# A grouped RMS norm whose factor is spread by a store to DRAM and a broadcast read, in place of matmuls with diagonals

## The chip, the cores and the metric

The kernel runs on one core of a Trainium2 chip. The metric is the device time of one execution in microseconds; the time of a kernel is the median of its runs. Smaller is better.

## The reference

The kernel is one step of a hybrid decoder trunk: an RMS norm of the input, one large input projection, two branches, a gated merge, an output projection, a residual and a last RMS norm. The change lies in branch A, a Mamba-2 state space branch (SSD) with 64 heads in 8 groups. Its output `y` is gated with `z`, normalised over the 512 channels of each group, and projected:

```python
def gated_group_rms_norm(y, z, w):
    g = y.astype(jnp.float32) * jax.nn.silu(z.astype(jnp.float32))
    shp = g.shape
    g = g.reshape(shp[:-1] + (SSD_GROUPS, shp[-1] // SSD_GROUPS))
    g = g * lax.rsqrt(jnp.mean(g * g, axis=-1, keepdims=True) + EPS)
    return (g.reshape(shp) * w.astype(jnp.float32)).astype(y.dtype)
...
    y = jnp.concatenate(ys, axis=1) + d_skip[:, None] * xs
    y = gated_group_rms_norm(y.reshape(bsz, length, D_INNER), z, ssd_norm_w)
    y_a = y @ w_ssd_out
```

There are 320 tokens that count (256 of the prompt and 8 x 8 samples) and 16 meta tokens ahead of them. For each group and each token one number, the factor 1/sqrt(mean + eps), multiplies all 512 channels.

## The kernel before, in words

Channels lie on the 128 partitions and tokens along the free dimension, so a group's `y` is four tiles `ys` of 128 x 320. The sum over 512 channels is a sum over four tiles and over partitions, and the factor, one number for each token, has to stand on all partitions.

**Projections.** Nearly all of TensorE's work (PE) is projections. A weight block of 128 x 1024 comes by DMA from SP (`wraw`, line 80), ACT rounds it to fp32r (`whi`, L82), DVE makes the remainder (`wlo`, L84), each in three buffers. `mm` (L90, L91, L94) then makes high by high, high by low and low by high products into a PSUM tile `pj`, of which there are two. A projection of the input takes two blocks, 48 matmuls into one `pj`; a block of the branch's own output projection (`out_units`, L563) serves two tiles of 12 matmuls, and each is added to `ya` by DVE (L574), which frees the `pj`.

**The weave.** For each group g a generator `ssd` makes the branch's small steps; it stops at each `yield`. `weave` (L594) runs the projections of the group's gate `z` (4 units), the output projection of group g−1 (8 units) and the convolution inputs of group g+1 (6 units) one after the other, and lets `ssd` advance between units so that NSTEP steps are spread over them; what is left runs at the end. Group 0 has no output projection to weave in, and group 7 has gate units (8) in place of the next group's convolutions. A scheduler then sets the order on each engine within what the buffers and the data allow. All engines run their instructions in order, and SP issues its DMAs in order too.

**One group's steps.** Three chunks of tokens (L436 to L518): transposes (L444), the decay weights `W` read from DRAM (L441) and worked by DVE (L456), the chunk's products (L475, L493, L470), the state (L504). In the third chunk the sampled states enter (L481, L483) and POOL multiplies eight states `h` with their decays (L486). Then `ys` is multiplied with the gate `zs` by DVE (L528), ACT squares it into `zs` (L529), POOL adds the four squares (L531). Two passes over the sampled states follow (L533 to L552): selections by matmuls (L535 to L541), state products (L548) in four `sg` tiles of which two buffers exist, added to `h` by DVE (L549) and stored (L551).

**The norm.** Last comes `rstd` (L106). It sums the squares over partitions for three spans of 112 tokens, each by a matmul with a column of ones (L112); DVE scales and adds eps (L116); POOL raises to −1/2 (L117); now each span's factors stand one to a partition. DVE multiplies the identity with them (three diagonals `rs_d`, L122), and a matmul of ones with each diagonal (L123) puts the factors on all partitions, in PSUM. DVE multiplies `ys` with weight and factor (L557), ACT rounds (`yh`, L558), DVE makes the remainder (`yl`, L559). The same `rstd` serves the first norm (L223) and the last (L646).

Of the kernel before, what the change touches and what calls it, by code (L numbers as in the profile page):

```python
# [7 lines left out]
F32 = mybir.dt.float32  # L8
F32R = mybir.dt.float32r
AF = mybir.ActivationFunctionType  # L10
ALU = mybir.AluOpType
PSUM = bass.MemoryType.PSUM

P = 128
T = 336
META = 16
TV = T - META
# [3 lines left out]
NG = 8  # L21
NH = 64
HP = 64
EPS = 1e-6
NSTEP = 25

C_ID, C_U, C_M1, C_UQ, C_M1Q, C_ONE = 0, 128, 256, 384, 464, 544
C_SX, C_SE, C_SY, C_SEG = 672, 1696, 1824, 1904
# [9 lines left out]
def bc(ap, shape):  # L38
    return ap.to_broadcast(shape)
# [3 lines left out]
def tile_hybrid_step(ctx, tc, xT, w1, w2, wdt, wso, wsc, wo, cmask, vec, hvec, convst, sconvst, h0T,  # L43
                     yT, convo, ssmp, ssms, sconvo):
    nc = tc.nc
    mult, add, sub = ALU.mult, ALU.add, ALU.subtract
# [3 lines left out]
    ps = ctx.enter_context(tc.tile_pool(name="ps", bufs=2, space=PSUM))  # L50
    dr = ctx.enter_context(tc.tile_pool(name="dr", bufs=1, space=bass.MemoryType.DRAM))

    ac_d = [dr.tile([NH, n], F32, name=f"ac_d{c}") for c, n in enumerate((P, P, 80))]
    mb_d = dr.tile([KT, P, TV], F32, name="mb_d")
    sg_d = dr.tile([KT, P, TV], F32, name="sg_d")

    V = keep.tile([P, V_ALL], F32, name="V")
    CR = keep.tile([P, C_ALL], F32R, name="CR")
# [9 lines left out]
    ones = CM[:, C_ONE:C_ONE + P]  # L68
# [3 lines left out]
    mhalf = keep.tile([P, 1], F32, name="mhalf")  # L72
# [33 lines left out]
    def rstd(pool, sums, t0, inv, eps):  # L106
        nt, w = T - t0, T // 3
        spans = [(a, a + w) for a in (0, w, nt - w)]
        pt_ = ps.tile([P, 512], F32, name="ms")
        for c, (a, b) in enumerate(spans):  # L110
            for i, sq in enumerate(sums):
                nc.tensor.matmul(pt_[:w, c:c + 1], sq[:, a:b], ones[:, 0:1],  # L112
                                 start=i == 0, stop=i == len(sums) - 1)
        m = pool.tile([P, 3], F32, name="rs_m", bufs=1)
        r = pool.tile([P, 3], F32, name="rs_r", bufs=1)
        nc.vector.tensor_scalar(m[:w], pt_[:w, 0:3], inv, eps, mult, add)  # L116
        nc.gpsimd.tensor_tensor(r[:w], m[:w], bc(mhalf[:w], [w, 3]), ALU.pow)  # L117
        yield
        pb_ = ps.tile([P, 512], F32, name="ms")
        for c, (a, b) in enumerate(spans):  # L120
            dg = pool.tile([P, P], F32, name="rs_d", tag="cbm", bufs=2)
            nc.vector.tensor_scalar(dg[:w, :w], ident[:w, :w], r[:w, c:c + 1], None, mult)  # L122
            nc.tensor.matmul(pb_[:, a:b], ones[:w, :], dg[:w, :w], start=True, stop=True)  # L123
        yield
        return pb_[:, :nt]
# [17 lines left out]
    with tc.tile_pool(name="pa", bufs=2) as pa:  # L143
# [19 lines left out]
        for half in range(2):  # L163
            for k in range(8):
                for i in range(2):
                    hi, lo = wb[i][half]
                    kk = 8 * half + k
                    for j, (w, x) in enumerate(((hi, uhi), (hi, ulo), (lo, uhi))):
                        nc.tensor.matmul(pu[i][:, :T - 14], w[:, k * P:k * P + P], x[:, kk, 14:],
                                         start=kk == 0 and j == 0, stop=kk == 15 and j == 2)  # L170
# [40 lines left out]
        for k in range(KT):  # L211
            sq = pa.tile([P, T], F32, name="sq") if k else sacc
# [10 lines left out]
        rs = run(rstd(pa, [sacc], 0, 1.0 / DM, EPS))  # L223
# [136 lines left out]
    with tc.tile_pool(name="pb", bufs=2) as pb:  # L360
# [61 lines left out]
        def ssd(g, st):  # L422
# [13 lines left out]
            for c, (t0, n) in enumerate(CH):  # L436
                um = U if c < 2 else UQ
                r = n if c < 2 else 16
# [51 lines left out]
                for t in range(4):  # L490
                    for q in range(2):
# [4 lines left out]
                                         start=t == 0, stop=t == 3 and c == 0)  # L496
# [29 lines left out]
            zs = st["zs"]  # L526
            for t in range(4):
                nc.vector.tensor_tensor(ys[t], ys[t], zs[t], mult)  # L528
                nc.scalar.activation(zs[t], ys[t], AF.Square)  # L529
                if t:  # L530
                    nc.gpsimd.tensor_tensor(zs[0], zs[0], zs[t], add)  # L531
            yield
            for u in range(2):  # L533
                pp = ps.tile([P, 512], F32, name="ms")
                nc.tensor.matmul(pp, sel(0, u), xeh[:80], start=True, stop=False)  # L535
                nc.tensor.matmul(pp, sel(1, u), xel[:80], start=False, stop=True)
                xh = big("xdt", 2, F32R)
                nc.scalar.activation(xh, pp, AF.Copy)
                pq = ps.tile([P, 512], F32, name="ms")
                nc.tensor.matmul(pq[:, 0:P], sel(2, u), bhh[:80, 0, :], start=True, stop=False)  # L540
                nc.tensor.matmul(pq[:, 0:P], sel(3, u), bhh[:80, 1, :], start=False, stop=True)  # L541
                bh = pb.tile([P, P], F32R, name="bh", bufs=1)
                nc.scalar.activation(bh, pq[:, 0:P], AF.Copy)
                yield
                yield
                for b in range(4):
                    pst = ps.tile([P, 512], F32, name="sg")
                    nc.tensor.matmul(pst, bh[32 * b:32 * b + 32, :], xh[32 * b:32 * b + 32, :], start=True, stop=True)  # L548
                    nc.vector.tensor_tensor(h0[4 * u + b], h0[4 * u + b], pst, add)  # L549
                    if b % 2:  # L550
                        nc.sync.dma_start(ssms[g, :, 4 * u + b - 1:4 * u + b + 1, :], h0t[2 * u + b // 2])  # L551
                        yield  # L552
            rs = yield from rstd(pb, [zs[0]], META, 1.0 / 512, 4.0 * EPS)
            yh = pb.tile([P, 4, TV], F32R, name="yh", bufs=1)
            yl = pb.tile([P, 4, TV], F32R, name="yl", bufs=1)
            for t in range(4):
                nc.vector.scalar_tensor_tensor(ys[t], ys[t], col(V_SNW, 4 * g + t), rs, mult, mult)  # L557
                nc.scalar.activation(yh[:, t, :], ys[t], AF.Copy)  # L558
                nc.vector.tensor_tensor(yl[:, t, :], ys[t], fb(yh[:, t, :]), sub)  # L559
            st["y"] = (yh, yl)  # L560
            yield

        def out_units(g, st):  # L563
            yh, yl = st["y"]
# [67 lines left out]
    with tc.tile_pool(name="pc", bufs=3) as pc_:  # L632
# [4 lines left out]
        for m in range(KT):  # L637
# [4 lines left out]
            sq = pc_.tile([P, TV], F32, name="sqf") if m else sacc  # L642
# [120 lines left out]
```

## Time and profile before

| what | before |
|---|---|
| median of 3 runs | 1926.32 us (1925.75 to 1926.34) |
| profiled execution, span (its own time) | 1925.9 us |
| PE busy | 1893.5 us, 98% |
| DVE busy | 1147.6 us, 60% |
| ACT busy | 754.1 us, 39% |
| POOL busy | 281.5 us, 15% |
| DMA moved | 318.66 MB, mean 165 GB/s |

How to read it: the span runs from the first to the last instruction of the one execution that was profiled. An f32 matmul shows as several records: x16 stands for eight matmuls, x6 for three. Ends of matmuls are modelled, so one record's duration reaches into the next; what a step costs PE is read from start to start. The line numbers are those of the kernel before; in the changed kernel a line stands one to fifteen lower down, and the text says which kernel it means where that matters.

### The profile page before, as it was taken

The page shows a single profiled execution, that of the slowest core. Times are in us where ns is not written, and L with a number is a line of the kernel's source. Part 1 is how long each engine was busy: PE and PEld are TensorE (multiplying, and loading weights), DVE is VectorE, ACT ScalarE, POOL GpSimd, SP SyncE. Part 2 cuts the span into 40 slices and gives each one's busy share as a digit, 9 for nine tenths or more (in the row PEclk, how much of TensorE's full clock was granted, in tenths as well). Part 3 has the DMA queues.
Part 4 walks back from the last instruction along what each step waited for, and adds up shares of the span by engine and source line. Part 5 has one row for each costly group of instructions (what it writes and reads, how often), then busy time and mean ns, then how long its engine had stood idle before and what let it go on. Part 6 is the DMA issues. An engine that isn't in the chain of part 4 may idle for free.

```text
span 1925.9 us, 31685 instructions
## 1 busy us (share of the span) xinstructions
PE 1893.5 (98%) x12742; PEld 1821.8 (95%) x12742; DVE 1147.6 (60%) x1839; ACT 754.1 (39%) x1066; POOL 281.5 (15%) x389
## 2 busy tenths in 40 slices
PE   7999999999999999999999999999999999999996
PEld 7999999999999999898998989989899898999996
DVE  7744444444543347776667777677676776564543
ACT  6433333333333335444433534435344352333431
POOL 0100000000000001413113131131311312100011
PEclk9999999999999999999999999999999999999998
DMA  6444444444444454363645536455364463564553
GB/s 234 148 166 148 149 148 148 153 145 155 148 158 152 158 203 163 130 205 119 230 142 184 172 124 230 136 179 177 131 228 138 165 204 115 193 226 166 169 176 106
DMA packets 100930, 318.66 MB, mean 165 GB/s; under 512 B 15920, under 2 KB 26800, under 8 KB 100784
## 3 DMA queue, kind: packets, MB, share of 16 engines
q1 hardware_dynamic: 100784, 316.65, 48.1%
q8 instruction: 100, 1.64, 0.3%
q14 instruction: 46, 0.38, 0.1%
HBM read 290.28 MB, written 26.32 MB: 164 GB/s over the span
## 4 chain that ended last, share of the span: by engine, by line
PE 64%; DVE 3%; DMA 1%; issue 0%; ACT 0%; POOL 0%; DVEq 0%; SPq 0%; ACTq 0%
PE pj L90 19%; PE pj L91 19%; PE pj L94 19%; PE sg L504 1%; PE yb L493 1%; PE yb L470 1%; PE sg L548 1%; PE ms L481 1%; DVE wlo L84 1%; DVE W L456 1%; DVE ys L528 1%; PE ms L444 1%; PE ms L123 0%; PE ms L475 0%; PE ms L483 0%; DMA W<-ac_d 0%
## 5 line engine op out<-in xcount | busy, mean ns | idle before, releaser
L84 DVE TENSOR_TENSOR wlo<-wraw,whi 128x1024 fp32r<-128x1024 f32 x481 | 595.7, 1239 | 534.6 <-PE pj L94 300.0
L90 PE MATMUL pj<-hhi,whi 128*128 128x320 f32 (+3 forms) x2960 | 895.0, 314 | 0.0
L91 PE MATMUL pj<-hlo,whi 128*128 128x320 f32 (+3 forms) x2960 | 888.5, 312 | 0.0
L82 ACT ACTIVATE whi<-wraw 128x1024 fp32r<-128x1024 f32 x481 | 509.3, 1059 | 936.9 <-PE pj L91 859.8
L90 PEld LDWEIGHTS pj<-hhi,whi 128*128 128x128 f32 x2960 | 556.8, 188 | 7.4 <-issue 6.9
L91 PEld LDWEIGHTS pj<-hlo,whi 128*128 128x128 f32 x2960 | 556.1, 188 | 0.8 <-issue 0.5
L94 PE MATMUL pj<-hhi,wlo 128*128 128x320 f32 (+3 forms) x2960 | 502.6, 312 | 0.0
L94 PEld LDWEIGHTS pj<-hhi,wlo 128*128 128x128 f32 x2960 | 456.3, 188 | 0.5 <-issue 0.2
L90 PE MATMUL pj<-yh,whi 128*128 128x320 f32 x512 | 160.0, 324 | 2.9 <-DVE ya L574 2.5
L91 PE MATMUL pj<-yl,whi 128*128 128x320 f32 x512 | 152.4, 309 | 0.0
L90 PEld LDWEIGHTS pj<-yh,whi 128*128 128x128 f32 x512 | 96.2, 188 | 20.5 <-issue 15.1
L91 PEld LDWEIGHTS pj<-yl,whi 128*128 128x128 f32 x512 | 96.3, 188 | 1.9 <-issue 1.9
L94 PE MATMUL pj<-yh,wlo 128*128 128x320 f32 x512 | 97.2, 310 | 0.0
L383 DVE SCALAR_TENSOR_TENSOR cacc<-pad,V,cacc 128x360 f32<-128x360 f32 (+1 forms) x144 | 86.3, 599 | 5.4 <-ACT cacc L381 1.4
L486 POOL TENSOR_TENSOR h<-h,decS 128x512 f32<-128x512 f32 x64 | 81.5, 1307 | 11.5 <-PE ms L481 11.4
L94 PEld LDWEIGHTS pj<-yh,wlo 128*128 128x128 f32 x512 | 80.4, 188 | 1.4 <-issue 1.4
L574 DVE TENSOR_TENSOR ya<-ya,pj 128x320 f32<-128x320 f32 x112 | 53.9, 482 | 42.3 <-PE pj L94 41.3
L377 POOL COPY CS<-pad 128x3 f32<-128x3 f32 x48 | 35.4, 737 | 279.3 <-ACT pad L374 279.3
L91 PE MATMUL pj<-vlo,whi 128*128 128x320 f32 x256 | 75.5, 309 | 0.0
L90 PE MATMUL pj<-vhi,whi 128*128 128x320 f32 x256 | 75.5, 309 | 0.0
L193 POOL COPY SCS<-up 128x2 f32<-128x2 f32 x16 | 20.5, 1280 | 369.2 <-DVE up L187 365.9
L456 DVE TENSOR_SCALAR W<-W,act 128x128 f32<-128x128 f32 (+1 forms) x192 | 46.5, 303 | 10.0 <-DMA W<-ac_d 10.0
(204 smaller groups left out, 1511.6 us busy)
## 6 DMA issues: line engine op xcount, KB each, us to landing
wraw<-w SPq DMA_DIRECT2D x352, 512.0 KB, 3.6
wraw<-wso SPq DMA_DIRECT2D x64, 512.0 KB, 3.5
wraw<-wsc SPq DMA_DIRECT2D x32, 512.0 KB, 3.6
h<-h0T SPq DMA_DIRECT2D x32, 512.0 KB, 6.1
ssms<-h SPq DMA_DIRECT2D x32, 512.0 KB, 4.2
wraw<-wo SPq DMA_DIRECT2D x32, 512.0 KB, 3.6
W<-ac_d SPq DMA_DIRECT2D x16, 512.0 KB, 6.2
mb_d<-thg SPq DMA_DIRECT2D x16, 160.0 KB, 1.8
```

The lines of the kernel that those rows point to most:

```text
L82: nc.scalar.activation(hi[:, :n], raw[:, :n], AF.Copy)
L84: nc.vector.tensor_tensor(lo[:, :n], raw[:, :n], fb(hi[:, :n]), sub)
L90: nc.tensor.matmul(out, w, xh(k0 + k), start=first and k == 0, stop=False)
L91: nc.tensor.matmul(out, w, xl(k0 + k), start=False, stop=False)
L94: nc.tensor.matmul(out, w, xh(k0 + k), start=False, stop=last and k == nk - 1)
L193: nc.gpsimd.tensor_copy(SCS[:, j, 0, :], up[:, 256:258])
L377: nc.gpsimd.tensor_copy(CS[:, j, 0, :], pad[:, 272:275])
L383: nc.vector.scalar_tensor_tensor(acc[:, i0:], pad[:, i0 + k:360 + k], col(V_CW, 4 * j + k), acc[:, i0:], mult, add)
L444: nc.tensor.transpose(pp[:n, t * P:t * P + P], xs[:, t, t0:t0 + n], ident)
L456: nc.vector.tensor_scalar(W[:n, h, :n], W[:n, h, :n], act[:n, c, 8 * g + h:8 * g + h + 1], 0.0, sub, ALU.min)
L486: nc.gpsimd.tensor_tensor(split(h0[b]), split(h0[b]), bc(hv(decS[:, b, :], g), [P, 8, HP]), mult)
L574: nc.vector.tensor_tensor(ya[:, m, :TV], ya[:, m, :TV], pp[:, :TV], add)
```

## The change

Of the grouped norm, the sums are made as soon as the squares are there, by a new generator `row_sums`: four spans of 80 tokens, each on 80 partitions. The factors (80 x 4, `rs_r`) are stored by SP to a DRAM tile of 320 floats for each group, one element at a time since a partition holds tokens that lie 80 apart; the norm at the end reads the 320 floats back to all 128 partitions (`rs`, 160 KB in SBUF). The diagonals and their matmuls are gone from the eight groups; the first and the last norm keep them. NSTEP goes from 25 to 23.

```diff
-NSTEP = 25
+NSTEP = 23
...
+    rs_d = [dr.tile([4, 80], F32, name=f"rs_d{g}") for g in range(NG)]
...
             yield
+            yield from row_sums(g, zs[0])
             for u in range(2):
                 pp = ps.tile([P, 512], F32, name="ms")
...
-            rs = yield from rstd(pb, [zs[0]], META, 1.0 / 512, 4.0 * EPS)
             yh = pb.tile([P, 4, TV], F32R, name="yh", bufs=1)
             yl = pb.tile([P, 4, TV], F32R, name="yl", bufs=1)
+            rs = pb.tile([P, TV], F32, name="rs", bufs=1)
+            nc.sync.dma_start(rs, rs_d[g].rearrange("c p -> (c p)").partition_broadcast(P))
             for t in range(4):
                 nc.vector.scalar_tensor_tensor(ys[t], ys[t], col(V_SNW, 4 * g + t), rs, mult, mult)
...
+        def row_sums(g, sq):
+            pt_ = ps.tile([P, 512], F32, name="ms")
+            for c in range(4):
+                nc.tensor.matmul(pt_[:80, c:c + 1], sq[:, 80 * c:80 * c + 80], ones[:, 0:1], start=True, stop=True)
+            m = pb.tile([P, 4], F32, name="rs_m", bufs=1)
+            r = pb.tile([P, 4], F32, name="rs_r", bufs=1)
+            nc.vector.tensor_scalar(m[:80], pt_[:80, 0:4], 1.0 / 512, 4.0 * EPS, mult, add)
+            nc.gpsimd.tensor_tensor(r[:80], m[:80], bc(mhalf[:80], [80, 4]), ALU.pow)
+            yield
+            with nc.allow_non_contiguous_dma(reason="one factor per token"):
+                nc.sync.dma_start(rs_d[g].rearrange("c p -> p c"), r[:80])
```

In the changed kernel the sums are L569, the scaling L572, the power L573, the store L576, the read L558, the products L560, `yl` L562, the add to `ya` L589, the state products L550, their adds L551 and their stores L553.

How the order moves is shown for a steady group. On PE, around the sums after (`yh`, `yl` are the group before's output, `zs` the squares):

```order
L95 MATMUL pj<-yh,wlo 128x320 x4
L569 MATMUL ms<-CR,zs 80x1 x4
L91 MATMUL pj<-yh,whi 128x320
L92 MATMUL pj<-yl,whi 128x320
L91 MATMUL pj<-yh,whi 128x320
```

Before, the sums stood behind both passes over the sampled states, among the next group's convolutions; now they stand ahead of the first pass, after 24 output projection matmuls that follow the state matmul L505.

On DVE, the norm before (`cacc` and `pad` are the next group's convolutions, `ms` the PSUM tile with the sums, `CR` holds the identity):

```order
L116 TENSOR_SCALAR rs_m<-ms 112x3
L383 SCALAR_TENSOR_TENSOR cacc<-pad_6689,V,cacc 128x360
L122 TENSOR_SCALAR rs_d<-CR,rs_r 112x112
L383 SCALAR_TENSOR_TENSOR cacc<-pad_6689,V,cacc 128x360
L122 TENSOR_SCALAR rs_d<-CR,rs_r 112x112
L383 SCALAR_TENSOR_TENSOR cacc<-pad_6689,V,cacc 128x360
L84 TENSOR_TENSOR wlo<-wraw,whi 128x1024
```

And on DVE after, from the sums' scaling to the products with the factor:

```order
L572 TENSOR_SCALAR rs_m<-ms 80x4
L85 TENSOR_TENSOR wlo<-wraw,whi 128x1024
L589 TENSOR_TENSOR ya<-ya,pj 128x320 x2
L85 TENSOR_TENSOR wlo<-wraw,whi 128x1024
L560 SCALAR_TENSOR_TENSOR ys<-ys,V,rs 128x320 x2
L589 TENSOR_TENSOR ya<-ya,pj 128x320
L560 SCALAR_TENSOR_TENSOR ys<-ys,V,rs 128x320 x2
L589 TENSOR_TENSOR ya<-ya,pj 128x320
L551 TENSOR_TENSOR h_10726<-h_10726,sg 128x512 x2
L85 TENSOR_TENSOR wlo<-wraw,whi 128x1024
```

The products with the factor now stand four instructions behind the scaling, with adds to `ya`, state adds and a weight remainder behind them.

On SP after (`ssmp`, `ssms` are states that go out):

```order
L81 DMA wraw<-w 128x1024
L512 DMA ssmp<-hst 128x512
L576 DMA rs_d_74<-rs_r 80x4x1
L81 DMA wraw<-w 128x1024
L558 DMA rs<-rs_d_74 128x320
L81 DMA wraw<-w 128x1024
L553 DMA ssms<-h_10726 128x1024
```

The store and the read are two new DMAs on SP, each with a weight load behind it.

## The prediction

> **What bounds the kernel now.** I read the top of the page first, then the shares of the chain that ended last.
>
> ```profile
> span 1925.9 us, 31685 instructions
> ...
> PE 1893.5 (98%) x12742; PEld 1821.8 (95%) x12742; DVE 1147.6 (60%) x1839; ACT 754.1 (39%) x1066; POOL 281.5 (15%) x389
> ...
> PE 64%; DVE 3%; DMA 1%; issue 0%; ACT 0%; POOL 0%; DVEq 0%; SPq 0%; ACTq 0%
> ```
>
> PE is busy for 98% of the span; the rest of the chain is other engines only where PE waits for them. So a step counts if it adds or takes PE instructions, changes a PE wait, or changes PE's clock. The chain of waits in order of time gives the rhythm: the sample product (L481) comes once in each group.
>
> ```profile
> 1017.98 1.85 PE ms L481 x16
> ...
> 1139.28 1.85 PE ms L481 x16
> ...
> 1260.59 1.85 PE ms L481 x16
> ```
>
> The period is 121.3 us (1260.59 − 1139.28) for each of groups 1 to 6; groups 0 and 7 have other units woven in and are taken apart below. One such period, by windows:
>
> ```profile
> core 0: us, PE busy (x) PEld busy (x) DVE busy (x) ACT busy (x) POOL busy (x), PEclk, DMA share, GB/s
> 1139.20:1260.50 121.30, 120.80 (x812) 112.38 (x811) 86.91 (x154) 50.38 (x78) 28.26 (x39) 1.00 0.50 169
> ```
>
> PE is idle for 0.50 us out of 121.30, at the full granted clock. There is next to nothing to win but PE's own instructions, and much room to lose. The timeline of PE, from L481 to the norm of the same group, has what the change touches:
>
> ```profile
> 1139.21 1.92 PE L481 MATMUL ms<-h,CZ 128*32 128x512 f32 x16
> ...
> 1152.04 0.39 PE L535 MATMUL ms<-xe,CR 80*128 80x512 f32 x1
> ...
> 1156.91 0.38 PE L90 MATMUL pj<-yh,whi 128*128 128x320 f32 x1 [0.50 <-DVE ya L574]
> ...
> 1160.60 0.50 PE L548 MATMUL sg<-xdt,bh 32*128 32x512 f32 x2
> 1161.02 0.42 PE L90 MATMUL pj<-yh,whi 128*128 128x320 f32 x1
> ...
> 1162.11 0.50 PE L548 MATMUL sg<-xdt,bh 32*128 32x512 f32 x1
> 1162.54 0.41 PE L90 MATMUL pj<-yh,whi 128*128 128x320 f32 x1
> ...
> 1189.81 0.66 PE L112 MATMUL ms<-CR,zs 128*112 128x1 f32 x6
> 1190.33 0.40 PE L90 MATMUL pj<-hhi,whi 128*128 128x336 f32 x1
> ...
> 1197.84 0.59 PE L123 MATMUL ms<-rs_d,CR 112*128 112x112 f32 x4
> 1198.20 0.40 PE L90 MATMUL pj<-hhi,whi 128*128 128x336 f32 x1
> ...
> 1199.57 0.47 PE L123 MATMUL ms<-rs_d,CR 112*128 112x112 f32 x2
> 1199.81 0.40 PE L90 MATMUL pj<-hhi,whi 128*128 128x336 f32 x1
> ```
>
> The 0.50 us is one wait of the projections for a PSUM buffer that DVE empties (L574). The norm's own matmuls cost PE, start to next start, 0.52 us (the sums), 0.36 and 0.24 us (the diagonals).
>
> **The change part by part, one group of 1 to 6.** Times are counted from L481's start, 1139.21.
>
> *Diagonals and sums.* The six diagonal matmuls and their two interruptions go: −0.60 us. The sums become four spans for three: 0.52 × 8/6 = 0.69, so +0.17. Together −0.43; with the short projection pieces beside the diagonals gone too, I take −0.5.
>
> *Fewer steps in the weave.* NSTEP 23 puts the state matmuls (L548, L550 after) in pairs between whole projection blocks; before, one pair was torn into two singles. By the rows a pair costs 0.42 (1160.60 to 1161.02) and a single 0.43 (1162.11 to 1162.54), so a pair in place of two singles saves 0.43, and the restarts of the projections (the first matmul 0.25 us from start to start, not 0.15) some 0.2 each: −0.83. The wait of 0.50 us goes if DVE is ahead there; in the new order all eight W steps stand before the row sums and no longer between the two adds that free the buffers. With its restart: −0.65. On the other side L471, L476 and L505 (before L470, L475 and L504) now stand alone at more places: about five restarts of 0.1, +0.5.
>
> *The sums move forward, and PE waits for POOL.* The four sums follow L505 and 24 projection matmuls; between L481 and them lie the same 48 projection matmuls that lay between L481 and L535, so PE comes to them at 1152.04 − 1139.21 = 12.83 us, with the new restarts at 12.9 to 13.0. They need the squares that POOL adds up:
>
> ```profile
> 1140.34 10.03 POOL L486 TENSOR_TENSOR h<-h,decS 128x512 f32<-128x512 f32 x8 [1.63 <-PE ms L481]
> 1151.70 3.00 POOL L531 TENSOR_TENSOR zs<-zs 128x320 f32<-128x320 f32 x3 [1.33 <-ACT zs L529]
> ...
> 1191.45 0.86 POOL L117 TENSOR_TENSOR rs_r<-rs_m,mhalf 112x3 f32<-112x3 f32 x1
> ```
>
> The decay products start 1.13 after L481 and take 10.03; then come the three additions, 3.00. Even if the squares are early (the 1.33 us of waiting goes, since the y sums L471 stand earlier), POOL is done at 1.13 + 10.03 + 3.00 = 14.2. So PE waits 14.2 − 13.0 = 1.2 us, at the most 1.4, where before nothing waited: the sums stood 38 us further on. This is the largest new cost, +1.2. Below it the cost goes to zero only if POOL's additions come ahead of the decay products, and they do not stand so in the order.
>
> Sum for one group: −0.5 − 0.83 − 0.65 + 0.5 + 1.2 = −0.28. Six groups: **−1.7 us**.
>
> *The factor's way through DRAM.* No run of before shows a write of single elements or a read of 4 × 80 floats to all partitions. The nearest rows, by issue to landing:
>
> ```profile
> W<-ac_d SPq DMA_DIRECT2D x16, 512.0 KB, 6.2
> mb_d<-thg SPq DMA_DIRECT2D x16, 160.0 KB, 1.8
> ...
> xr<-xT SPq DMA_DIRECT2D x16, 160.0 KB, 2.2
> ...
> ys<-mb_d SPq DMA_DIRECT2D x16, 160.0 KB, 3.7
> ...
> ac_d<-acT SPq DMA_DIRECT2D x1, 20.0 KB, 5.1
> ```
>
> The near pair (a store of 1.8, a load of the same 160 KB of 2.2) makes 4.0 us; the far pair (5.1 and the 6.2 of the broadcast W, which carries three times the bytes) make 11.3. What is free: from the first sum to the power's start it was 1191.45 − 1189.81 = 1.64, the power 0.86, so the write is issued at 14.2 + 1.64 + 0.86 + 0.3 = 17.0. On DVE the first two ys products wait for the factor, and behind them in DVE's queue stands the ya add that frees the PSUM buffer for the projection block after the first state pair; behind that the h adds and the next wlo. PE comes to that block after 48 matmuls, the selections (L537 to L543) and the pair: 14.2 + 0.7 + 3.6 + 0.64 + 3.6 + 0.43, at 23.2 to 23.4. One DVE pass over 128x320 takes:
>
> ```profile
> 1149.54 2.38 DVE L528 TENSOR_TENSOR ys<-ys,zs 128x320 f32<-128x320 f32 x4
> ...
> L574 DVE TENSOR_TENSOR ya<-ya,pj 128x320 f32<-128x320 f32 x112 | 53.9, 482 | 42.3 <-PE pj L94 41.3
> ```
>
> Two products at 2.38/4 = 0.6, at the least 0.54, and one add of 0.48 make 1.6 us, so the factor has to land by 21.7: a round trip of up to 4.7 us costs nothing, and each us beyond costs PE one us, six times. I take the near pair, 4.0: the loads of 160 KB come in 2.2 where nothing waits with them, and a store of 160 KB in 1.8. Cost 0, bounds 0 and (11.3 − 4.7) = 6.6 us a group. On SP, the write waits for POOL and the read for the write; behind them stand the wraw loads of the second and third block of the next unit. Their buffers come free only with wlo passes at 17 and 20 us, so the first loses nothing and the second at most 1 us out of a lead of two blocks (7 us).
>
> A rule speaks against this change: the Trainium skill, "DMA: Bandwidth & Descriptors", section "Rules for kernel authors", says that an access whose last dimension is not contiguous becomes one descriptor per element, here 320 of 4 bytes; the page puts no time on them, and no run of before shows such a transfer. By the same page's "Anatomy of one DMA — SWDGE (gpsimd) path", about 2.0 us are fixed in every DMA on the path that it measured, so two in a row would be an estimate of 4.0 us, still under 4.7; the 1.8 of the store row lies a little below that rule, so the trace about agrees, and the sum stays what it is by either.
>
> **Group 0.** There the wait is another one:
>
> ```profile
> 800.48 1.12 PE L504 MATMUL sg<-xe,bt 16*128 16x512 f32 x2
> ...
> 807.57 3.61 POOL L531 TENSOR_TENSOR zs<-zs 128x320 f32<-128x320 f32 x3 [3.10 <-ACT zs L529]
> ...
> 825.99 1.07 DVE L456 TENSOR_SCALAR W<-W,act 128x128 f32<-128x128 f32 x5 [4.21 <-DMA W<-ac_d]
> ...
> 829.92 0.49 PE L548 MATMUL sg<-xdt,bh 32*128 32x512 f32 x1 [2.16 <-DVE h L549]
> ```
> ```profile
> core 0: us, PE busy (x) PEld busy (x) DVE busy (x) ACT busy (x) POOL busy (x), PEclk, DMA share, GB/s
> 831.00:837.40 6.40, 6.40 (x21) 5.76 (x21) 4.01 (x7) 2.96 (x6) 0.60 (x3) 0.50 0.91 312
> ```
>
> DVE stood 4.21 us at a W step, the h add was queued behind it, and PE waited 2.16 us for that add; after it the granted clock is 0.50 for 6.4 us of this window (6.8 by the first and last slow matmuls), which costs 3.4. In the new order the h adds stand ahead of these W steps: −2.16 − 0.3 − 3.4 = −5.9, and the norm −0.5. But the sums come 48 matmuls (7.3 us) after L505, at 801.5 + 7.3 = 808.8, while POOL was done with the additions at 811.2: a wait of 2.4. The nearest row, 2.16, halved the clock; so will this, I take it: +2.4 + 3.4, +0.7 for one more torn pair, and 0.1 of restarts. Group 0: +0.2. In group 7 the sums stand 24 projection matmuls (3.6 us) later, at 16.5, past POOL's 14.2: no wait; two more singles +0.8, norm −1.0: −0.2.
>
> Total −1.7 + 0.2 − 0.2 = −1.7: a span of 1924.2. The profiled execution of before took 1925.9, the median of the runs shown is 0.4 above it, so the **forecast is 1924.6 us**.
>
> **The rivals.**
>
> *The wait of 2.4 us in group 0 leaves the clock alone.* Then 3.4 us less: 1921.2. For it: 1.04 us of waiting near the end of the kernel did not halve it.
>
> ```profile
> 1909.30 0.36 PE L112 MATMUL ms<-CR,sqf 128*112 128x1 f32 x2 [1.04 <-ACT sqf L643]
> ```
> ```profile
> core 0: us, PE busy (x) PEld busy (x) DVE busy (x) ACT busy (x) POOL busy (x), PEclk, DMA share, GB/s
> 1909.30:1912.70 3.40, 1.84 (x14) 1.58 (x14) 0.86 (x4) 0.00 (x0) 0.86 (x1) 1.00 0.00 0
> ```
>
> Against it: 2.16 us did, once. But it is one case, and nothing here shows a second wait of that length. I give it 0.25. The Trainium skill, "TensorE: Matmul & The Clock Gate", section "Part 1: The HAM clock gate (the “warmup” mystery)", has the clock fall only after an idle window of about 3.4 us, by which no wait in this sum would halve it; the row of 2.16 us disagrees.
>
> *The factor comes late: slower.* Its place is the ys product on DVE, with the ya add behind it; it decides from a round trip of 4.7 us on. With two transfers of 3.7 us, as the ys<-mb_d row, the trip is 7.4: 2.7 or 2.8 us in each of six groups, +17, about 1941; with 5.2 us, +3, about 1928. For it: all transfers share the queues with 512-KB loads, and 320 elements of 4 bytes are unlike any row. Against: the two near rows. 0.17.
>
> *The six waits of 1.2 us halve the clock:* 6 × 3.4 = +20, 1945. The row of 1.04 us speaks against it. 0.07.
>
> *POOL's additions are early, or the wait is not there:* 6 × 1.2 = 7.2 less, 1917. The scheduler's order puts the decay products first; that they are faster than the row has no support. 0.12.
>
> *The weave saves nothing:* the torn pair's and the buffer wait's 1.48 us come back elsewhere in every group, +8.9, 1933.5. 0.05.
>
> **How the numbers follow.** The forecast has 0.34, the rivals 0.25, 0.17, 0.07, 0.12 and 0.05. A measurement of this kernel can tell 0.2%, 3.85 us: faster is below 1922.5, slower above 1930.2. Faster: 0.25 + 0.12 and a little of the forecast's spread, 0.38. Slower: 0.05 + 0.07 + most of the 0.17 less what its lower end leaves within the bound, 0.24. No difference: the rest, 0.38. The range goes from 1916 (no wait in the six groups) to 1936, the late factor with a round trip of 6.6 us: (6.6 − 4.7) × 6 = 11.4 above 1924.6. Left out are the far ends of the late factor and the halved clock in all groups, together under 0.2. The likeliest case by itself runs from 1922.5 to 1927.
>
> **What would show it right or wrong.** In the timeline of PE after: a wait of 1.2 to 1.4 us ahead of L569, released by POOL, in groups 1 to 6, and about 2.4 in group 0, followed by a slice at a clock of 0.50; a period of L482 of 121.0; no wait at the block after L543; no 0.50 wait on ya. In the DMA issues: rs_d<-rs_r and rs<-rs_d together under 4.7 us. The prediction is wrong if L560's products are released by the DMA later than 21.7 after L482 and PE waits for ya behind them, if the clock falls in the steady groups, or if the period grows.

## The result, and the profile after

The changed kernel takes 2001.01 us (median of 4 runs, 1999.68 to 2004.12), the kernel before, run beside it, 1926.33 us (4 runs, 1925.75 to 1928.71). The ratio is 1.0384 with an interval of 1.0372 to 1.0397: 75 us slower, where 1924.6 was forecast and 1936 was the top of the range. The profiled execution has a span of 1997.5 us, 71.6 more than before; the account below is made on the spans.

The top of the page of the changed kernel, its chain by engine, and two groups of instructions (after the bar: busy us, mean ns of one; after the second bar the idle time of the engine ahead of them and what ended it):

```profile
span 1997.5 us, 31597 instructions
...
PE 1906.8 (95%) x12710; PEld 1834.7 (92%) x12710; DVE 1157.8 (58%) x1815; ACT 755.1 (38%) x1066; POOL 291.8 (15%) x389
...
PE 59%; DMA 5%; DVE 4%; POOL 1%; issue 1%; ACT 0%; DVEq 0%; ACTq 0%
...
L91 PE MATMUL pj<-hhi,whi 128*128 128x320 f32 (+3 forms) x2960 | 905.5, 317 | 41.8 <-DVE ya L589 38.3
...
L560 DVE SCALAR_TENSOR_TENSOR ys<-ys,V,rs 128x320 f32<-128x320 f32 x32 | 16.1, 548 | 72.7 <-DMA rs<-rs_d 72.7
```

PE is busy 13.3 us longer with fewer instructions, which is the clock (windows below), and idle 58.3 us longer (71.6 − 13.3). DMA has gone from 1% to 5% of the chain. DVE stood 72.7 us ahead of the eight groups' products with the factor, nearly all of it unseen by the busy shares, and the projections waited 38.3 us for adds to `ya`. The issues of the store and of the read, with KB and us from issue to landing:

```profile
rs<-rs_d SPq DMA_DIRECT2D x8, 160.0 KB, 5.2
...
rs_d<-rs_r SPq DMA_DIRECT2D x8, 1.2 KB, 7.4
```

That is a trip (from the store's issue to the read's landing) of 12.6 us, where the prediction took 4.0 and set the free length at 4.7. In one steady group the timelines show all of it; SP, POOL, DVE and PE in this order:

```profile
1048.44 1.93 POOL L573 TENSOR_TENSOR rs_r<-rs_m,mhalf 80x4 f32<-80x4 f32 x1 [1.41 <-DVE rs_m L572]
```
```profile
1050.39 0.33 SPq L576 DMA_DIRECT2D rs_d<-rs_r  x1
1050.81 0.42 SPq L81 DMA_DIRECT2D wraw<-w  x1
1057.59 0.32 SPq L558 DMA_DIRECT2D rs<-rs_d  x1
```
```profile
1062.78 1.01 DVE L560 SCALAR_TENSOR_TENSOR ys<-ys,V,rs 128x320 f32<-128x320 f32 x2 [9.53 <-DMA rs<-rs_d]
1063.71 0.48 DVE L589 TENSOR_TENSOR ya<-ya,pj 128x320 f32<-128x320 f32 x1
```
```profile
1043.85 0.41 PE L91 MATMUL pj<-yh,whi 128*128 128x320 f32 x1 [0.72 <-DVE ya L589]
...
1047.08 0.73 PE L569 MATMUL ms<-CR,zs 128*80 128x1 f32 x8 [1.20 <-POOL zs L532]
...
1055.57 0.50 PE L550 MATMUL sg<-xdt,bh 32*128 32x512 f32 x2
...
1064.25 0.65 PE L91 MATMUL pj<-hhi,whi 128*128 128x336 f32 x1 [8.18 <-DVE ya L589]
```

Read it backwards. PE stops behind the first state pair for 8.18 us, at the block that the prediction named. It is released by the second row of DVE, an add of 0.48 us that had nothing to wait for itself; it stood in the queue behind two products, and these waited 9.53 us for the read. SP issued the read as soon as the store had landed, 7.20 us after its issue. Windows over the wait and the time after it show the granted clock (the last three columns are clock, DMA share, GB/s):

```profile
core 0: us, PE busy (x) PEld busy (x) DVE busy (x) ACT busy (x) POOL busy (x), PEclk, DMA share, GB/s
1055.80:1064.40 8.60, 0.42 (x3) 0.15 (x1) 1.62 (x4) 1.27 (x3) 0.00 (x0) 0.62 0.58 128
1064.40:1068.30 3.90, 3.90 (x15) 3.90 (x16) 3.90 (x8) 0.93 (x2) 0.00 (x0) 0.52 0.19 78
```

The clock fell inside the wait and was still at half speed for 3.9 us behind it, which costs 1.9 us more. The period from L482 to L482 grew accordingly:

```profile
1032.11 1.85 PE ms L482 x16
...
1163.68 1.85 PE ms L482 x16
```

131.57 us against 121.30, 10.27 more. The late factor and its clock are 8.18 + 1.9, the wait for POOL ahead of the sums is 1.20; that is 11.3. The wait at an add to `ya` is 0.72 in place of 0.50, and PE's work without the slow clock is 119.6 us (121.47 busy in this period, less 1.9) in place of 120.80, 1.2 less.

Group 1 is an experiment that the program makes by itself. There `out_units` makes group 0's output, which ACT copies (L587), so no add to `ya` stands on DVE:

```profile
938.89 1.94 DVE L560 SCALAR_TENSOR_TENSOR ys<-ys,V,rs 128x320 f32<-128x320 f32 x4 [7.50 <-DMA rs<-rs_d]
```

DVE waits 7.50 us all the same, and PE does not wait for it at all.

### The profile page after: what moved, and what is told of

It reads as the page before. It is cut to its first block, busy times and chain, and to the rows that moved or that the text cites. A ratio compares the mean times of both kernels' runs of the same rounds, so it can differ in the third digit from the quotient of the medians.

```text
span 1997.5 us, 31597 instructions
## 1 busy us (share of the span) xinstructions
PE 1906.8 (95%) x12710; PEld 1834.7 (92%) x12710; DVE 1157.8 (58%) x1815; ACT 755.1 (38%) x1066; POOL 291.8 (15%) x389
## 2 busy tenths in 40 slices
DMA packets 104769, 319.98 MB, mean 160 GB/s; under 512 B 18736, under 2 KB 30640, under 8 KB 104624
## 4 chain that ended last, share of the span: by engine, by line
PE 59%; DMA 5%; DVE 4%; POOL 1%; issue 1%; ACT 0%; DVEq 0%; ACTq 0%
PE pj L91 18%; PE pj L92 17%; PE pj L95 17%; DMA rs_d<-rs_r 3%; DMA rs<-rs_d 2%; DVE W L457 1%; PE yb L494 1%; DVE ys L529 1%; PE yb L471 1%; PE sg L505 1%; PE ms L482 1%; PE sg L550 1%; POOL rs_r L573 1%; PE ms L445 1%; DVE wlo L85 0%
## 5 line engine op out<-in xcount | busy, mean ns | idle before, releaser
L91 PE MATMUL pj<-hhi,whi 128*128 128x320 f32 (+3 forms) x2960 | 905.5, 317 | 41.8 <-DVE ya L589 38.3
L85 DVE TENSOR_TENSOR wlo<-wraw,whi 128x1024 fp32r<-128x1024 f32 x481 | 588.5, 1224 | 517.9 <-PE pj L95 270.6
L91 PEld LDWEIGHTS pj<-hhi,whi 128*128 128x128 f32 x2960 | 563.5, 190 | 55.6 <-DVE ya L589 39.9
L92 PEld LDWEIGHTS pj<-hlo,whi 128*128 128x128 f32 x2960 | 563.0, 190 | 3.0 <-issue 2.6
L91 PE MATMUL pj<-yh,whi 128*128 128x320 f32 x512 | 165.2, 334 | 4.9 <-DVE ya L589 3.6
L378 POOL COPY CS<-pad 128x3 f32<-128x3 f32 x48 | 41.3, 861 | 303.6 <-ACT pad L375 303.6
L487 POOL TENSOR_TENSOR h<-h,decS 128x512 f32<-128x512 f32 x64 | 79.2, 1270 | 11.8 <-PE ms L482 11.8
L589 DVE TENSOR_TENSOR ya<-ya,pj 128x320 f32<-128x320 f32 x112 | 54.1, 483 | 43.4 <-PE pj L95 43.0
L560 DVE SCALAR_TENSOR_TENSOR ys<-ys,V,rs 128x320 f32<-128x320 f32 x32 | 16.1, 548 | 72.7 <-DMA rs<-rs_d 72.7
```

The lines of the kernel that those rows point to most:

```text
L85: nc.vector.tensor_tensor(lo[:, :n], raw[:, :n], fb(hi[:, :n]), sub)
L91: nc.tensor.matmul(out, w, xh(k0 + k), start=first and k == 0, stop=False)
L92: nc.tensor.matmul(out, w, xl(k0 + k), start=False, stop=False)
L378: nc.gpsimd.tensor_copy(CS[:, j, 0, :], pad[:, 272:275])
L487: nc.gpsimd.tensor_tensor(split(h0[b]), split(h0[b]), bc(hv(decS[:, b, :], g), [P, 8, HP]), mult)
L589: nc.vector.tensor_tensor(ya[:, m, :TV], ya[:, m, :TV], pp[:, :TV], add)
```

## The experiments

Theory A: the trip is waited for on DVE, and what is queued behind the products stops PE. Theory B: SP is what is held, with weight loads behind its two new waits. Theory C: the early sums and the weave of 23 steps cost it. A fourth, D, came out of the runs and is given there. Each ratio is against runs of the kernel before on the same chip.

**The products pinned to the group's end.** They are the same instructions, queued on DVE behind all that stands ahead of them in the program:

```diff
-                nc.vector.scalar_tensor_tensor(ys[t], ys[t], col(V_SNW, 4 * g + t), rs, mult, mult)
+                tc.keep_in_program_order(
+                    nc.vector.scalar_tensor_tensor(ys[t], ys[t], col(V_SNW, 4 * g + t), rs, mult, mult))
```

> The four products with the factor (L560) are pinned on DVE behind everything traced before them, so they stand at the end of the group; store, read, early sums and NSTEP 23 stay as in the changed kernel. Theory A (the factor's trip of 12.6 us, waited for on DVE with the ya add and the h adds queued behind): the 9 us of idle DVE ahead of L560 and the waits of 8 to 9 us on PE go, and with them the stretches of half clock that follow; the time is 1921 to 1930 us. Theory B (SP is what is held: weight loads stand behind the store's wait and the read's wait): PE waits of several us stay, now released by ACT's or DVE's work on weights; 1950 us or more. Theory C (the early sums and the weave of 23 cost it): as the changed kernel, 1990 us or more.

Measured: 1942.31 us, ratio 1.0086 (1.0070 to 1.0101). The store still takes 7.4 us and the read 5.9. DVE's row of the products, and the two groups of PE in which the waits for `ya` and for POOL stand:

```profile
L561 DVE SCALAR_TENSOR_TENSOR ys<-ys,V,rs 128x320 f32<-128x320 f32 x32 | 18.2, 570 | 0.0
...
L91 PE MATMUL pj<-yh,whi 128*128 128x320 f32 x512 | 164.6, 332 | 4.9 <-DVE ya L590 3.6 <-ACT ya L588 1.2
...
L570 PE MATMUL ms<-CR,zs 128*80 128x1 f32 x64 | 5.8, 212 | 7.4 <-POOL zs L532 7.4
```

72.7 us of idle DVE are 0.0, PE is busy 1895.0 us in place of 1906.8, and 58.7 of the 75 us are back (2001.0 − 1942.3). So the place of the products in DVE's queue, not the trip as such, made most of the loss, as A has it. But the run is 12 us above A's band, so something else costs as well.

**Early sums, factor spread by diagonals** (four of 80x80, at the group's end; no store, no read):

```diff
+            for c in range(4):
+                dg = pb.tile([P, P], F32, name="rs_g", tag="cbm", bufs=2)
+                nc.vector.tensor_scalar(dg[:80, :80], ident[:80, :80], st["r"][:80, c:c + 1], None, mult)
+                nc.tensor.matmul(rs[:, 80 * c:80 * c + 80], ones[:80, :], dg[:80, :80], start=True, stop=True)
```

> Early sums over four spans of 80 and NSTEP 23 stay, but the factor stays on the chip: four diagonals of 80x80 and four matmuls spread it, at the end of the group; no store, no read. Theories A and B: 1922 to 1932 us (the changed kernel's weave and sums with the old way of spreading, which costs about 0.7 us more on PE in each group than the DRAM way would). Theory C (early sums and weave cost it): 1990 us or more.

Measured: 1938.93 us, 1.0062 (1.0047 to 1.0077). Without the store and the read, sums and weave still cost 12 us over before (7.5 of it are waits of the sums for POOL): C is wrong for the bulk, but not for a rest of 12 us that A and B had put at 6 at the most.

**Four neighbouring tokens on a partition.** The sums take every fourth column, so that the store is 16 bytes from each partition into one run:

```diff
-                nc.tensor.matmul(pt_[:80, c:c + 1], sq[:, 80 * c:80 * c + 80], ones[:, 0:1], start=True, stop=True)
+                nc.tensor.matmul(pt_[:80, c:c + 1], sq.rearrange("p (q c) -> p c q", c=4)[:, c, :], ones[:, 0:1], start=True, stop=True)
...
-                nc.sync.dma_start(rs_d[g].rearrange("c p -> p c"), r[:80])
+            nc.sync.dma_start(rs_d[g], r[:80])
```

> As the changed kernel, but a partition holds four neighbouring tokens (the sums take every fourth column), so the store writes 16 bytes from each partition to one unbroken run of 1280 bytes in place of 320 single floats. If the single elements make the store slow, it falls from 7.4 us to the 2 to 4 us of the other stores, the trip to 7 to 9 us, PE's wait to 3 to 5 us in groups 2 to 6, and the time to 1945 to 1970 us. If the store is slow because of what else is under way on the queues or in DRAM, it stays at 6 to 8 us and the time at 1995 to 2005 us.

Measured: 1945.96 us, 1.0111 (1.0090 to 1.0132). The issues and the group of the products:

```profile
rs<-rs_d SPq DMA_DIRECT2D x8, 160.0 KB, 4.6
...
rs_d<-rs_r SPq DMA_DIRECT2D x8, 1.2 KB, 1.4
```
```profile
L560 DVE SCALAR_TENSOR_TENSOR ys<-ys,V,rs 128x320 f32<-128x320 f32 x32 | 16.1, 547 | 18.3 <-DMA rs<-rs_d 18.3
...
L91 PE MATMUL pj<-hhi,whi 128*128 128x320 f32 (+3 forms) x2960 | 897.3, 314 | 5.3 <-DVE ya L588 5.3
```

The same 1.2 KB land in 1.4 us in place of 7.4: the single floats made the store slow, not the load on the queues. The trip is 6.0 us, and PE's wait at the block falls from 38.3 us to 5.3. That is the threshold tried from nearby: the trip is a little too long, and the wait is between nothing and 3.00 us in the five groups 2 to 6. The new sums are dearer, though: with every fourth column they cost PE 4.8 us more in the whole run, 10.4 against 5.6 in two runs further down with the same order. Each comparison of the short store with single floats has this in it.

**NSTEP back at 25**, all else as changed (one number in the diff).

> The changed kernel with NSTEP back at 25. Theory A: the products with the factor stand at the same place of the DVE queue and wait for the same trip, so 1990 to 2008 us. If the weave of 23 steps is what costs (theory C): 1926 to 1950 us.

Measured: 2006.11 us, 1.0410 (1.0394 to 1.0425). The weave of 23 steps is not what costs here; with 25 the changed kernel is even 5.1 us slower (2006.1 − 2001.0).

**NSTEP 23 in the kernel before** (one number in the diff).

> The kernel before with nothing changed but NSTEP 23: sums over three spans and diagonals at the end of the group, as before. It measures the weave alone. By the prediction's terms for it (a torn pair and a 0.50 us wait less, some restarts more: about -1.0 us in each of six groups, and the 2.16 us wait with its stretch of half clock in group 0) it is 1914 to 1921 us. If the new weave makes waits of its own (0.8 us at a ya add, as seen ahead of the early sums in the run with diagonals), 1925 to 1933 us.

Measured: 1932.49 us, 1.0028 (1.0018 to 1.0037). In the kernel before, the weave alone is a loss, at the top of the second band. Its chain has a period of 122.1 us (1265.66 − 1143.53), and the waits at the adds to `ya` have moved and grown, not gone. The second fence shows them on PE, the third the products with the gate on DVE:

```profile
1143.53 1.85 PE ms L481 x16
1265.66 1.85 PE ms L481 x16
```
```profile
1155.25 0.42 PE L90 MATMUL pj<-yh,whi 128*128 128x320 f32 x1 [0.72 <-DVE ya L574]
...
1158.12 0.38 PE L90 MATMUL pj<-yh,whi 128*128 128x320 f32 x1 [0.19 <-DVE ya L574]
```
```profile
1150.38 3.43 DVE L528 TENSOR_TENSOR ys<-ys,zs 128x320 f32<-128x320 f32 x3
1153.74 1.06 DVE L456 TENSOR_SCALAR W<-W,act 128x128 f32<-128x128 f32 x1
1154.72 0.47 DVE L574 TENSOR_TENSOR ya<-ya,pj 128x320 f32<-128x320 f32 x1
```

L470 comes earlier in this weave, so the products with the gate now fall into POOL's 10 us of decay products. There they take 3.43 / 3 = 1.14 us each (0.60 before, when POOL was nearly done), a W step 1.06 (0.30 on the mean), and the add to `ya` that PE waits for stands behind them. In this period PE idles 1.05 us in place of 0.50 and is busy 0.3 us longer (121.08 against 120.80).

**Sums behind the first pass over the states**, short store, products pinned, NSTEP 23:

```diff
-            yield from row_sums(g, zs[0])
             for u in range(2):
...
                         yield
+                if u == 0:
+                    yield from row_sums(g, zs[0])
```

> The factor's way through DRAM with both mends (16 bytes from each partition in one run, products pinned to the group's end), NSTEP 23, and the sums moved behind the first pass over the sampled states, so that POOL is done when PE comes to them. If the early sums' wait for POOL is what is left in the run with the pinned products, its 1.27 us in each of six groups goes: 1930 to 1936 us, or 1922 to 1930 if group 0's stretch of half clock goes with it. If the rest has another cause (the weave, the later DVE work), it stays at 1938 to 1943 us.

Measured: 1927.73 us, 1.0000 (0.9991 to 1.0009). No matmul of the sums waits for POOL any more. The last run below differs from this one in the place of the sums alone and takes 1938.86: their early place is some 11 us (1938.9 − 1927.7), 7.4 of which are waits for POOL.

**Sums at their old place, factor through DRAM, NSTEP 25**, first with single floats, then with the short store. The only differences to before are the four spans and the way of spreading:

```diff
-            rs = yield from rstd(pb, [zs[0]], META, 1.0 / 512, 4.0 * EPS)
+            yield from row_sums(g, zs[0])
...
+            nc.sync.dma_start(rs, rs_d[g].rearrange("c p -> (c p)").partition_broadcast(P))
```

> The store and the read alone: NSTEP 25 and the sums at the place that they had before, among the next group's convolutions, only the diagonals are gone; single floats as in the changed kernel. Theory A: the trip is again 12 to 13 us, some 5.5 us of DVE work on the convolutions stands between the scaling and the first product, so DVE idles for 5 to 7 us a group; no ya add is queued behind it there, but convolution adds and the weight remainders (wlo) are, with two blocks of lead, so PE waits 2 to 5 us a group: 1940 to 1965 us. If only the ya add behind the products made PE wait, nothing does here: 1923 to 1930 us. If the trip's length itself falls where no ssmp store and no W load are near, also 1923 to 1930 us, with a trip under 8 us in the trace.

> The same with four neighbouring tokens on a partition, so that the store is one run of 1280 bytes: a trip of about 6 us as seen with that store, which the 5.5 us of DVE work between cover but for a rest: 1921 to 1930 us by theory A, by which the difference to the run with single floats is the trip's alone. If something else than the trip holds DVE there, both take the same.

Measured: 1953.00 us, 1.0130 (1.0114 to 1.0145), with single floats; 1925.96 us, 0.9992 (0.9982 to 1.0001), with the short store. The trips are 9.5 + 5.1 and 4.1 + 4.1 us, DVE's idle time ahead of the products 50.3 and 3.3 us. Both fit A; that single floats also hold up loads, as found further down, is not separated here. The short store saves 27 us although its sums are dearer, and the way through DRAM is then as fast as the diagonals.

**Nothing waits for the factor**: NSTEP 25, sums between the two passes, products pinned; once with the short store, once with single floats. The order on DVE is the same, row by row; the sums differ as said above.

```diff
                 bh = pb.tile([P, P], F32R, name="bh", bufs=1)
                 nc.scalar.activation(bh, pq[:, 0:P], AF.Copy)
+                if u:
+                    yield from row_sums(g, zs[0])
                 yield
```

> NSTEP 25, the sums between the two passes over the sampled states (PE comes there well after POOL's additions), one run of 1280 bytes for the store, and the products pinned to the group's end, some 40 us after the store. By theory A nothing waits for the trip, and the early sums cost no wait: the period is 121.0 us or a little less, as in the run with the sums at the end and the short store, without that run's 3.3 us of idle DVE: 1921 to 1926 us. If the later place of the products or of their rounding costs DVE or ACT time that PE waits for, 1928 to 1935 us.

> The same with the single floats of the changed kernel, so that the trip is 12 us or more again, and the DVE order is the same row by row. Theory A (only a trip that someone waits for costs): the same time as with the short store, within 2 us. If the 320 single elements also disturb the weight loads on the DMA queues, or hold SP with the next weight load behind the read's wait, it is slower by 3 us or more, with PE waits on weights (whi or wlo) in the trace.

Measured: 1925.21 us, 0.9989 (0.9980 to 0.9997), with the short store, the fastest of all, 2 us under the kernel before; 1950.55 us, 1.0118 (1.0102 to 1.0133), with single floats. The 2 us do not come from the norm: the steady period is 121.5 us in place of 121.3, and the gain stands in group 0, 102.5 us from its sample product to the next in place of 106.4, where PE's wait of 2.16 us and the half clock behind it are gone. For the single floats A fails: no engine waits for the factor, and they cost 25 us, or 30 if the dearer sums of the short store are counted. SP's timeline in one group, first with the short store, then with single floats:

```profile
1164.94 0.34 SPq L577 DMA_DIRECT2D rs_d<-rs_r  x1
...
1172.56 0.44 SPq L442 DMA_DIRECT2D W<-ac_d  x1
```
```profile
1176.48 0.33 SPq L578 DMA_DIRECT2D rs_d<-rs_r  x1
...
1183.62 2.27 SPq L559 DMA_DIRECT2D rs<-rs_d  x1
...
1187.39 0.67 SPq L442 DMA_DIRECT2D W<-ac_d  x1
```

The load of `W` is issued 7.6 us after the store with the one, 10.9 with the other, and lands 6.2 and 9.7 us after its issue; three weight loads issued just behind the store land in 5.3 to 5.9 and in 9.1 to 11.9 us. DVE's idle time ahead of the W steps is 22.1 and 44.3 us, the h adds are queued behind them, and PE waits 12.4 us for these where it did not before. So there are two suspects: the single floats hold up the loads by themselves (D), or SP is held at the read (B).

**Single floats, but the read takes the factor of the group before** (so the output is scaled by the wrong factor), so that SP does not stand at it. Group 0 has no group before it and reads its own factor, so there SP still does:

```diff
-            nc.sync.dma_start(rs, rs_d[g].rearrange("c p -> (c p)").partition_broadcast(P))
+            nc.sync.dma_start(rs, rs_d[max(g - 1, 0)].rearrange("c p -> (c p)").partition_broadcast(P))
```

> The run with the single floats and the pinned products (1950.6 us), but the read takes the factor of the group before (its output is not the reference's), so SP does not stand at the read for the store of the same group; the store of 320 single floats stays. Theory D (the single floats hold up the loads that are issued around them, by themselves): 1940 to 1951 us, weight loads issued just behind the store still land 9 to 12 us later. Theory B (SP stands at the read, with the W load and the weight loads behind it): 1925 to 1930 us, and the loads land in 4 to 6 us.

**Short store, and single floats that nobody reads**, as a second store behind it:

```diff
             nc.sync.dma_start(rs_d[g], r[:80])
+            with nc.allow_non_contiguous_dma(reason="320 single floats that nobody reads"):
+                nc.sync.dma_start(rs_x[g].rearrange("c p -> p c"), r[:80])
```

> The best run so far (1925.2 us: one run of 1280 bytes, read from there, products pinned, sums between the passes) with a second store behind the first: the same factors as 320 single floats into a DRAM tile that nobody reads. Nothing waits for it. Theory D: 1940 to 1951 us, loads behind it land 9 to 12 us after issue. Theory B: 1925 to 1928 us, since SP only issues one more DMA of 0.33 us.

Measured: 1931.53 us, 1.0021 (1.0011 to 1.0031), with the stale read; 1951.74 us, 1.0120 (1.0102 to 1.0138), with the extra store. The issues of the second:

```profile
rs<-rs_d SPq DMA_DIRECT2D x8, 160.0 KB, 10.9
...
rs_d<-rs_r SPq DMA_DIRECT2D x8, 1.2 KB, 1.4
rs_x<-rs_r SPq DMA_DIRECT2D x8, 1.2 KB, 8.0
```

The extra store alone brings 26.5 us (1951.7 − 1925.2), with the same sums in both runs and no wait of SP for its landing. The read, which waits for the short store only, lands after 10.9 us in place of 5.3, and three weight loads behind it after 7.9 to 11.8. That shows that single floats cost by themselves, as D has it; the time is just above D's band. The run with the stale read fits neither band. In a steady group the weight loads land just as late (9.7 to 11.3 us), yet the run is only 6.3 us above the one with the short store (1931.5 − 1925.2), or 11 if the dearer sums are counted. Its loss stands in group 0, where SP does wait at the read: from that group's sample product to the next it takes 111.6 us, like the 110.4 with the read in its place, against 102.5 with the short store. The steady groups take 120.9 us, and PE waits 0.3 us for h adds in the whole run, in place of 12.4. In these the read has gone from its place and the load of `W` stands one weight load further ahead on SP: it is issued 9.1 us after the store and lands 7.8 later, 16.9 us behind the store in all, against 20.6 with the pinned products and the read in its place. Whether the delay reaches PE thus hangs on the order on SP as well. So both suspects are real: taking SP's wait at the read out of seven groups gives back 19.0 us (1950.6 − 1931.5), as B has it, and single floats without that wait can cost 26.5, as D has it. How the 30 us divide between the held-up loads, the order on SP and its wait is not settled.

**Early sums and pinned products as in the first run, with the short store.**

> The run with early sums, NSTEP 23 and pinned products (1942.3 us), now with the short store; DVE's order is the same row by row. Theory D: what the single floats cost the loads at this place goes, and the time comes to that of the early sums with diagonals (1938.9 us) less some 0.3 us a group for the diagonals: 1934 to 1938 us. Theory B or no effect at this place: within 2 us of 1942.

Measured: 1938.86 us, 1.0054 (1.0038 to 1.0070), between the two bands, 3.4 under the run with single floats and level with the diagonals at the same place. The dearer sums are 4.8 us of it, so at the changed kernel's own place the held-up loads may cost up to some 8 us beside the trip. This is not sharp: in two of the five steady groups of this run the clock fell behind the wait for POOL (periods of 123.9 and 123.8 us against 122.2 to 122.6), and how often that happens differs from run to run.

Of the 75 us one part is firm: the place of the products in DVE's queue, 58.7 (2001.0 − 1942.3). The rest, some 15 us, does not come apart into fixed parts. The early place of the sums is 11 with the short store and 6.4 with the diagonals (1938.9 − 1932.5); the weave of 23 steps is a loss of 4.7 in the kernel before (1932.5 − 1927.8) and a gain of 5.1 in the changed one; the held-up loads are between 3.4 and 8.

## Why the prediction was wrong, point by point

**The factor's way through DRAM is the step that failed.** The prediction wrote "I take the near pair, 4.0" and "Cost 0". The trip is 12.6 us. The threshold beside it nearly held: 4.7 us were said to be free, and in the group shown it is 4.2 (the trip there is 12.4, from 1050.39 to 1062.78, and PE waits 8.18). With a trip of 6.0 PE waits 5.3 us in all, with 12.6 it waits 38.3 at the place that was named. What misled was that the nearest rows were chosen by their bytes. The store at 1.8 us moves 160 KB in whole rows; this store moves 1.2 KB as 320 elements, and no row of before resembled it. The far pair, 5.1 + 6.2 = 11.3 us, was written down and lay nearer, and by it the prediction's own bound was 6.6 us a group, 40 in all; yet the range stopped at a trip of 6.6 us. With no row of the kind, the far end belonged in the range. Even the far pair gives only about 1964 us: the measured trip is longer still, and the half clock behind the waits and the wait in group 0 were in no bound.

The rule that was set against the sum, from the Trainium skill ("DMA: Bandwidth & Descriptors", section "Rules for kernel authors": a last dimension that is not contiguous becomes one descriptor per element), is borne out. The page of the profile counts 18736 packets under 512 B in the run with single floats and pinned products and 16816 in its twin with the short store, 240 a store, which is 320 less 80. In time that is 7.4 us against 1.4.

**The rival "the factor comes late" was this mechanism**, at 0.17 and 1941 us. Its mechanism and place were right, its trip of 7.4 us was too short; and the half clock behind long waits, 1.9 us in the group shown, was left out of its price.

**The wait for POOL** was forecast at 1.2 to 1.4 us; it is 1.20. That is partly luck: PE comes to the sums 13.8 us behind L482, not 13.0, and POOL is done at 15.0, not 14.2, so two misses of 0.8 us cancel (PE had already waited 0.72 at `ya`, and POOL's three additions took 3.75 in place of 3.00, in the group shown). The rival that these waits halve the clock, at 0.07, came true in part. In two of the five steady groups of the changed kernel the granted clock is 0.50 soon behind the wait (1181 to 1184 and 1444 to 1447 us), in the other three it stays at 1.00; in the run with diagonals the windows behind five of these waits read 1.00.

**The weave** was forecast at −0.83 − 0.65 + 0.5, about −1.0 us a group. Alone it is +0.8 (122.1 against 121.3), which is the rival "the weave saves nothing", at 0.05. The wait of 0.50 us at the add to `ya` did not go: now the products with the gate stand ahead of that add on DVE, slowed beside POOL, and it is 0.72. PE's work did not fall either (121.08 against 120.80 us). The prediction had looked only for the W steps there, and had taken DVE's durations from a place where POOL was nearly done. The Trainium skill, "SBUF — State Buffer", section "SBUF: two separate sides", has DVE operations with two SBUF inputs and GpSimd take turns on one pair of ports, each for a whole instruction; 1.14 us in place of 0.60 beside POOL's decay products of about 1.3 us each agrees with it.

**The norm** was put at −0.5 us a group, which is about right. With the stale read, where the sums read neighbouring columns and the steady groups wait as before, the period is 120.9 against 121.3. With the short store and the sums at the old place it is 121.0 (1260.39 − 1139.41 in that run's chain), with the dearer sums in it.

**Group 0**: the wait of 2.16 us for `W` went, as said, and the wait for POOL is 0.56, not 2.4. In their place PE waits 8.34 us for an h add behind the products with the factor. **Group 7**, put at no wait, waits 3.50 us for a weight (`whi`) and 1.47 for an h add.

**SP** was priced at next to nothing, at most 1 us of the weight loads' lead. That the store would slow the loads behind it was not in the sum: in the group shown the weight load behind it lands 11.0 us after its issue, where the median of all is 3.8. Within the eight groups PE waits for a weight only in group 7.

**The clock.** In the sum a wait of 2.4 us halves it and one of 1.2 does not. The length of the wait alone does not decide it here: 1.20 did in two groups and did not in three, and 2.16 did in the kernel before and did not with NSTEP 23 in it (PE idle up to 914.2 us, granted clock 1.00 from there to 926). With 8.18 the granted clock is 0.62 over the wait and 0.52 behind it. The Trainium skill, "TensorE: Matmul & The Clock Gate", section "Part 1: The HAM clock gate (the “warmup” mystery)", names an idle window of about 3.4 us; the long waits agree with it, and the 2.16 us of the kernel before and the two waits of 1.20 stay against it.

## What to carry to other kernels

Price a transfer by how many separate pieces it has, not by its bytes, and if no row of the trace has its shape, keep the far bound in the range. Ask what stands behind the waiting instruction on its engine: the same trip cost 59 us more where adds that free PSUM were queued behind it than where the products were pinned to the group's end. A layout in which a partition holds neighbouring tokens made the store one run; with the consumer late, the kernel was then 0.1% faster than the one before (0.9989, 0.9980 to 0.9997), and that came from group 0, since the dearer sums took back what the norm saved.

## What the runs showed of the hardware

A store of 320 single floats holds up others: in one group of the run with the extra store the loads issued behind it land after 7.9 to 12.7 us, in place of 5.3 to 6.8 in its twin without that store, though nothing waits for it; the whole run is 26.5 us longer (1951.7 against 1925.2). SP itself is held: in the run with the extra store, issuing the second state load behind it took this long, where the same load took 0.43 us in its twin.

```profile
1183.64 5.91 SPq L433 DMA_DIRECT2D h<-h0T  x1
```

Some DVE instructions are slower beside POOL: 1.14 us for a product of 128x320 that takes 0.60 when POOL is nearly done; the adds to `ya`, which read one input from PSUM, are not (0.47 there as elsewhere). Sums that read every fourth column of an f32 tile are dearer for PE: 64 records take 10.4 us with the stride and 5.6 without in the two runs with the same order.
